# First mixer of a two-layer block: scans in a fixed tensor-engine order of fourteen steps, convolution evictions recorded ahead of the step

## The chip, the cores and the metric

The kernel runs on one NeuronCore of a Trainium2 chip. The metric is the device time of one execution in microseconds (us). The profile names the engines PE (TensorE, matmuls), PEld (its weight loads), DVE (VectorE), ACT (ScalarE), POOL (GpSimd) and SP (SyncE, here only a queue that issues DMAs).

## What is computed

The reference is a block of two layers: a state-space mixer, then an attention mixer, each followed by a mixture of experts. The change lies in the state-space mixer alone, which works on 512 latent tokens and 256 context tokens (T = 768, six chunks of 128; chunks 0 to 3 are latent, 4 and 5 context):

```
z, xbc, dtr = split(u @ in_w)                    # input projection
xbc = silu(conv5(xbc));  xs, Bm, Cm = split(xbc) # centred convolution of 5 taps
dt  = softplus(dtr + dt_bias);  acum = cumsum(dt * A)       # per chunk and direction
y_diag = ((Cm Bm^T) * exp(acum_l - acum_s) * tri) @ (dt * xs)
states = Bm^T @ (exp(acum_end - acum) * dt * xs)
h      = exp(acum_end) * h + states               # from chunk to chunk
y      = y_diag + (Cm * exp(acum)) @ h_prev       # forward and backward, summed
out    = rmsnorm((y + D * xs) * silu(z)) @ out_w
```

There are 8 groups of 4 heads, of 64 values each, and a forward and a backward scan in every group.

## The kernel before

`ssd` runs eight groups. For each, `ssd_in` projects six column tiles of 128 (B, C, x0, x1, z0, z1). A tile's fp32 weights come by DMA (SP), are split into a high part (`split`, L445, ACT) and a low part (L446, POOL), and `mm3` (L475 to L477) issues three matmuls for each of 8 slices of the input: 24 matmuls of 256 columns for the context half (PSUM tile `pin`), then 24 of 512 for the latent half. `pin` takes three PSUM banks in turn, so the first half of a tile can only start when the half tile three places earlier has been evicted. The eviction of B, C, x0 and x1 is the convolution: one ACT activation (L808) and four dependent DVE operations (L813) per half, then a tanh (L814) and a product (L816). z0 and z1 need one tanh and one DVE operation per half.

While group g+1 is projected, the scan of group g advances. `ssd_group` is a Python generator; `between`, called twice a tile, lets it run to its next `yield` and in every second call also runs one step of a filler (L544: eight matmuls for the modulation vectors, in groups 0 to 3 until they are used up). The generator's parts are `transposed(c)` (rows of x and B of a chunk by PE transposes, copied by ACT into `rowx`), `state(i)` (PE matmul into `st`, new state `hst` by DVE), `prepare(c)` (decay matrices: DMA `ab`, POOL L865, DVE L867, ACT exp L868 give `m`; `ce` is the decayed C; the PE product `cb` is masked into `cbm` by DVE L877 and L878, weighted by ACT L882 and DVE L883 and multiplied by `m` in L884, giving `w`), `product(c)` (24 or 16 small matmuls into the PSUM tile `y`, L902) and `ssd_out` (L945 and L946 on DVE, then a DMA).

The order of instructions on each engine is made by the framework's scheduler from the order of recording and its own estimates; the kernel fixes the order on PE only in other stages. After the eighth group the scan of the last group runs beside the context part of the output projection `ssd_proj`.

Of the kernel before, what the change touches and what calls it, by code (L numbers as in the profile page):

```python
# [22 lines left out]
P = 128  # L23
D = 1024
KT = 8
S = 512
# [353 lines left out]
class Kern:  # L380
# [225 lines left out]
    def ssd(self, e0, esc, rest):  # L606
# [7 lines left out]
        with ExitStack() as so:  # L614
# [13 lines left out]
            k = {nm: kp.tile([P, 6, 64], F32, name=nm) for nm in ("dt", "dtd", "acum", "dec")}  # L628
# [17 lines left out]
            inner = iter(())  # L646

            def between(i):
                next(inner, None)
                if i % 2:  # L650
                    next(filler, None)

            for g in range(8):
                cz = self.ssd_in(g, wp, gp, pp, (hhi, hlo), k, between)
                if g == 0:
                    self.ssd_dt(gp, wp, pp, (hhi, hlo), k, aS)
                for _ in inner:
                    pass
                inner = self.ssd_group(g, gp, pp, k, *cz)
# [9 lines left out]
            for n, _ in enumerate(inner):  # L669
                if n:  # L670
                    next(proj)
# [26 lines left out]
    def ssd_dt(self, tp, wp, pp, h, K, aS):  # L698
# [3 lines left out]
        dt, dtd, acum, dec, tle, tge = (K[n] for n in ("dt", "dtd", "acum", "dec", "tle", "tge"))  # L702
# [37 lines left out]
        nc.scalar.copy(acum, pa)  # L740
        pt = pp.tile([P, 6, 64], F32, name="ptot", tag="y")
# [19 lines left out]
    def ssd_in(self, g, wp, gp, pp, h, K, between):  # L761
# [20 lines left out]
        for i, nm in enumerate(names):  # L782
            if i in early:
                between(False)
                between(True)
# [3 lines left out]
            for a, b in ((S, T), (0, S)) if i not in early else ():  # L789
# [5 lines left out]
                between(a == 0)  # L795
            th = gp.tile([P, T], F32, name="th", tag="th", bufs=1)
            if nm[0] == "z":
                z = gp.tile([P, T], F32, name="zs", tag="zs", bufs=4)
                for p_, a, b, n in seg:
                    nc.scalar.activation(th[:, a:b], p_, AF.Tanh, scale=0.5)  # L800
                    nc.vector.scalar_tensor_tensor(z[:, a:b], th[:, a:b], 1.0, p_, op0=ALU.add, op1=ALU.mult)
                zs[nm] = z
                continue
            ct = ctile[nm]
            tap = lambda j: cwh[:, j * 32 + ct:j * 32 + ct + 1]
            acc = gp.tile([P, T], F32, name="acc", tag="acc", bufs=2)
            for p_, a, b, n in seg:
                nc.scalar.activation(acc[:, a:b], p_, AF.Identity, scale=tap(2), bias=cwh[:, 160 + ct:161 + ct])  # L808
                for j in (0, 1, 3, 4):
                    s = j - 2  # L810
# [9 lines left out]
    def ssd_group(self, g, gp, pp, K, conv, zs):  # L820
# [84 lines left out]
        for c in (4, 5, 0):  # L905
            transposed(c)
# [1555 lines left out]
```

## Time and profile before

| | |
|---|---|
| runs | 3304.07, 3310.75, 3310.1 us; median 3310.1 us |
| profiled execution | 3311.26 us, of which the span of the core is 3309.5 us |
| groups 0 to 7 of the mixer, from the first input matmul | 36.1 to 679.9 us of the span |
| tail of the mixer, last scan beside the context projection | 679.9 to about 773 us |

In the rows below a "form" is the shape of an instruction, `x` a count; "busy" is the union of the intervals, "mean ns" the length of one instruction, and "idle before" the time its engine waited and for whom. Matmul lengths overlap; the distance between two starts is what one costs.

### The profile page before, as it was taken

Reading aid. Unit: us, or ns where it says so; the run is one execution under the profiler, and the core shown is the slowest. Engines: PE = TensorE matmul, PEld = TensorE weight load, DVE = VectorE, ACT = ScalarE, POOL = GpSimd, SP = SyncE. Lnnn points to the kernel's source line nnn. Section 1 sums busy time; section 2 is a strip of 40 time slices with the busy share of each in tenths; the row PEclk is TensorE's granted clock in tenths of the full one; section 3 lists DMA queues with packets and bytes.
Section 4 is the critical chain, followed back from the end, with each engine's and each line's share of the span. In section 5 each row is a group of like instructions: output and inputs, shape, how many; then the busy total and the mean of one; then the engine's idle time right before and its main releaser. Section 6 shows DMA issues by size and latency. Waiting matters only on the chain.

```text
span 3309.5 us, 47859 instructions
## 1 busy us (share of the span) xinstructions
PE 3129.0 (95%) x18944; PEld 2070.5 (63%) x18944; DVE 1638.5 (50%) x3014; ACT 1165.6 (35%) x2063; POOL 965.6 (29%) x694
## 2 busy tenths in 40 slices
PE   7999998889999999999999899999999999999998
PEld 4677777777754343434757644434467778988886
DVE  5588888887522121114466410004379864763312
ACT  4344444455511111114567410001154354662222
POOL 1344545554210000002601200000154443145543
PEclk9999999989999999999999999999999999999999
DMA  7355433355488989894252589999832224443332
GB/s 253 125 165 163 143 89 92 101 163 163 127 304 329 358 323 369 318 367 148 83 185 67 219 326 409 409 400 398 324 118 80 80 65 150 134 158 100 96 92 86
DMA packets 234416, 668.60 MB, mean 202 GB/s; under 512 B 19344, under 2 KB 73488, under 8 KB 229840
## 3 DMA queue, kind: packets, MB, share of 16 engines
q1 hardware_dynamic: 224240, 645.43, 54.2%
q10 hardware_dynamic: 9952, 20.12, 1.9%
q8 instruction: 149, 2.44, 0.3%
q14 instruction: 75, 0.61, 0.1%
HBM read 651.65 MB, written 13.83 MB: 201 GB/s over the span
## 4 chain that ended last, share of the span: by engine, by line
PE 60%; DVE 8%; DMA 5%; ACT 2%; issue 2%; POOL 1%; SPq 0%; DVEq 0%; ACTq 0%; POOLq 0%
PE mm L475 7%; PE mm L476 7%; PE mm L477 7%; PE py L1102 3%; PE pg L1102 3%; PE pa L1102 3%; PE pa L1313 3%; PE py L1266 3%; PE pg L1313 2%; DMA wm<-in_moe_w_dram 2%; PE gth L343 2%; PE cy L1104 2%; PE cg L1104 2%; PE ca L1104 2%; DMA raw<-in_moe_w_dram 1%
## 5 line engine op out<-in xcount | busy, mean ns | idle before, releaser
L446 POOL TENSOR_TENSOR wlo<-raw,whi 128x1024 fp32r<-128x1024 f32 (+3 forms) x207 | 461.2, 2230 | 634.3 <-ACT whi L445 600.9
L445 ACT CAST whi<-raw 128x1024 fp32r<-128x1024 f32 (+2 forms) x291 | 285.7, 984 | 477.7 <-PE mm L476 200.8
L475 PE MATMUL mm<-stk,whi 128*128 128x512 f32 (+2 forms) x944 | 342.6, 363 | 0.0
L477 PE MATMUL mm<-stk,wlo 128*128 128x512 f32 (+2 forms) x944 | 335.9, 356 | 0.0
L476 PE MATMUL mm<-stk,whi 128*128 128x512 f32 (+2 forms) x944 | 335.1, 355 | 0.0
L475 PE MATMUL pin<-hhi,whi 128*128 128x256 f32 (+1 forms) x768 | 271.2, 354 | 4.0 <-DVE acc L813 3.8
L477 PE MATMUL pin<-hhi,wlo 128*128 128x256 f32 (+1 forms) x768 | 265.2, 345 | 0.0
L476 PE MATMUL pin<-hlo,whi 128*128 128x256 f32 (+1 forms) x768 | 263.3, 343 | 0.0
L58 POOL TENSOR_TENSOR sqa<-sqa,sq 128x256 f32<-128x256 f32 (+1 forms) x56 | 64.7, 1155 | 467.6 <-PE py L1266 408.5
L475 PEld LDWEIGHTS mm<-stk,whi 128*128 128x128 f32 (+1 forms) x944 | 179.7, 190 | 33.1 <-issue 7.9
L1166 POOL TENSOR_TENSOR cT<-cT,scc 128x256 f32<-128x256 f32 x56 | 39.6, 738 | 544.5 <-ACT scc L1165 543.7
L476 PEld LDWEIGHTS mm<-stk,whi 128*128 128x128 f32 (+1 forms) x944 | 179.6, 190 | 29.9 <-issue 6.2
L477 PEld LDWEIGHTS mm<-stk,wlo 128*128 128x128 f32 (+1 forms) x944 | 179.3, 190 | 26.1 <-issue 1.1
L475 PEld LDWEIGHTS pin<-hhi,whi 128*128 128x128 f32 x768 | 146.4, 191 | 45.9 <-issue 19.6
L1188 DVE TENSOR_TENSOR ac<-ac,pg 128x512 f32<-128x512 f32 x16 | 11.0, 687 | 300.4 <-PE pg L1102 300.4
L476 PEld LDWEIGHTS pin<-hlo,whi 128*128 128x128 f32 x768 | 146.5, 191 | 18.7 <-issue 1.7
L477 PEld LDWEIGHTS pin<-hhi,wlo 128*128 128x128 f32 x768 | 146.3, 190 | 18.3 <-issue 1.7
L813 DVE SCALAR_TENSOR_TENSOR acc<-pin,cwh,acc 128x511 f32<-128x511 f32 (+3 forms) x256 | 148.5, 608 | 14.3 <-ACT acc L808 12.6
L1345 DVE TENSOR_TENSOR ac<-ac,pg 128x512 f32<-128x512 f32 x16 | 11.0, 687 | 248.1 <-PE pg L1313 248.1
L867 DVE SCALAR_TENSOR_TENSOR m<-ab,acum,m 128x128 f32<-128x128 f32 x192 | 115.3, 643 | 25.3 <-POOL m L865 25.3
L446 DVE TENSOR_TENSOR wlo<-raw,whi 128x1024 fp32r<-128x1024 f32 (+1 forms) x84 | 105.0, 1254 | 40.7 <-ACT whi L445 40.0
L872 POOL TENSOR_TENSOR ce<-ce,xc 128x1024 f32<-128x1024 f32 (+1 forms) x48 | 103.4, 2154 | 39.8 <-ACT ce L871 36.0
(716 smaller groups left out, 7184.7 us busy)
## 6 DMA issues: line engine op xcount, KB each, us to landing
wm<-in_moe_w_dram SPq DMA_DIRECT2D x227, 1024.0 KB, 9.5
raw<-in_moe_w_dram SPq DMA_DIRECT2D x186, 512.0 KB, 8.9
raw<-in_ada_w_dram SPq DMA_DIRECT2D x96, 512.0 KB, 4.8
raw<-in_moe_w2h_dram SPq DMA_DIRECT2D x76, 512.0 KB, 8.9
raw<-in_w_f_dram SPq DMA_DIRECT2D x68, 512.0 KB, 3.6
wm<-in_moe_w2h_dram SPq DMA_DIRECT2D x26, 1024.0 KB, 8.3
raw<-in_w_ssd_in_dram SPq DMA_DIRECT2D x48, 512.0 KB, 4.6
ab<-aS SPq DMA_DIRECT2D x96, 256.0 KB, 4.7
```

The costliest lines, as they stand in the source:

```text
L445: nc.scalar.copy(hi[:, 0:n], raw[:, 0:n])
L446: (eng or self.lo).tensor_tensor(lo[:, 0:n], raw[:, 0:n], hi[:, 0:n].bitcast(F32), op=ALU.subtract)
L475: nc.tensor.matmul(ps, wh, ah, start=start, stop=False)
L476: nc.tensor.matmul(ps, wh, al, start=False, stop=False)
L477: nc.tensor.matmul(ps, wl, ah, start=False, stop=stop)
L813: nc.vector.scalar_tensor_tensor(o, p_[:, lo + s:hi + s], tap(j), o, op0=ALU.mult, op1=ALU.add)
L867: nc.vector.scalar_tensor_tensor(m[:, r, :], ab[:, r, :], acum[:, c, 4 * g + r:4 * g + r + 1], m[:, r, :], op0=ALU.subtract, op1=ALU.min)
L872: nc.gpsimd.tensor_tensor(ce[:, j0:j1, :], ce[:, j0:j1, :], conv["C"][:, o:o + P].unsqueeze(1).to_broadcast([P, j1 - j0, P]), op=ALU.mult)
L1102: nc.tensor.matmul(pb[z][o:o + 32, :], lb(k, e)[:, 32 * h:32 * h + 32], w[e][k % 2][:, z * 512:(z + 1) * 512], tile_position=(0, o), **f)
L1104: nc.tensor.matmul(pc[o:o + 32, :], ls(k, e), w[e][k % 2][:, h * 512:(h + 1) * 512], tile_position=(0, o), **f)
L1266: nc.tensor.matmul(py[64 * e:64 * e + 64, :], aT[:, k, 64 * e:64 * e + 64], w[e][a], start=(k == 0), stop=(k == KT - 1), tile_position=(0, ...
L1313: nc.tensor.matmul(pb[hf][64 * e:64 * e + 64, :], lb(k, e), w[e][a][:, hf * 512:(hf + 1) * 512], tile_position=(0, 64 * e), **f)
```

## The change

- The scan has fourteen steps. The first twelve run beside the next group's six tiles, the last two beside the first tile of the group after that, so `inner` is a list of generators. In groups 1 to 7 PE's order is that of recording (`manual_schedule`). Fillers stand at steps 1, 3, 5, 7, 9 and 11.
- A tile's eviction is recorded ahead of the step behind its latent half; before, both steps of a tile were recorded ahead of it.
- `prepare` becomes `begin` for two chunks together: (4, 5), (1, 2), (0, 3). Their products stand three or four steps later.
- Work moves from DVE to ACT: of the four L867 per chunk the subtraction becomes four ACT activations with a pointer bias, in place in `ab`, and one `tensor_tensor` of 512 columns takes the minimum. The state's eight products per step become eight ACT copies of 64 columns with a pointer scale (`hsc`), and both directions are added in one DVE operation of 512 columns. `cbm` is masked for two chunks at once.
- `nacum` (the negated `acum`) is computed once. The scaled rows `xdd` are made one step ahead of their state.

```diff
+            def scans():
+                for z in list(inner):
+                    if next(z, inner) is inner:
+                        inner.remove(z)
+
+            def between():
+                nonlocal step
+                scans()
+                if step in FILL:
                     next(filler, None)
+                step += 1
...
+                with tc.manual_schedule(engines={mybir.EngineType.PE}) if g else ExitStack():
+                    cz = self.ssd_in(g, wp, gp, pp, (hhi, hlo), k, between)
...
-                inner = self.ssd_group(g, gp, pp, k, *cz)
+                inner.append(self.ssd_group(g, gp, pp, k, *cz))
...
+            scans()
+            while inner:
+                scans()
+                next(proj)
...
-                between(a == 0)
...
+                if a:
+                    between()
+            self.ssd_evict(nm, seg, ctile.get(nm), gp, cwh, conv, zs)
+            between()
...
+            hn = gp.tile([P, 512], F32, name="hst", tag="hst", bufs=5)
...
+                nc.vector.tensor_tensor(hn, hsc[0], ps, op=ALU.add)
...
+                    nc.scalar.activation(hsc[0][:, o:o + 64], hn[:, o:o + 64], AF.Copy, scale=dec[:, c, col:col + 1])
...
             for r in range(4):
-                nc.vector.scalar_tensor_tensor(m[:, r, :], ab[:, r, :], acum[:, c, 4 * g + r:4 * g + r + 1], m[:, r, :], op0=ALU.subtract, op1=ALU.min)
+                nc.scalar.activation(ab[:, r, :], ab[:, r, :], AF.Identity, bias=nacum[:, c, 4 * g + r:4 * g + r + 1])
+            nc.vector.tensor_tensor(m, ab[:, 0:4, :], m, op=ALU.min)
...
+            for z, t in enumerate((tle, tge)):
+                nc.vector.tensor_tensor(cb[:, z], p2, t.unsqueeze(1).to_broadcast([P, 2, P]), op=ALU.mult)
...
+        transposed(4)
+        transposed(5)
         yield
+        transposed(0)
+        transposed(3)
+        scaled(0)
+        yield
         state(0)
+        begin(4, 5)
+        scaled(1)
         yield
         state(1)
+        scaled(2)
+        transposed(1)
         yield
+        transposed(2)
+        yield
+        product(4)
+        product(5)
         state(2)
+        begin(1, 2)
+        yield
+        self.ssd_out(g, gp, yctx, S, C, conv, zs)
+        scaled(3)
         yield
         state(3)
+        scaled(4)
         yield
         state(4)
         yield
+        product(1)
+        product(2)
+        begin(0, 3)
         yield
+        yield
+        yield
         yield
         product(0)
         product(3)
         self.ssd_out(g, gp, ylat, 0, S, conv, zs)
```

PE in group 1, where the step sizes have just been computed (`ptot` ends that computation, `st` is the first state of the first scan). Before:

```order
L738 MATMUL pa<-dt_la,tle 128x6x32
L739 MATMUL pa<-dt_la,tge 128x6x32
L742 MATMUL ptot<-dt_la,ones 128x384
L477 MATMUL pin<-hhi,wlo 128x256
L475 MATMUL pin<-hhi,whi 128x256
```

After:

```order
L746 MATMUL pa<-dt_la,tle 128x6x32
L747 MATMUL pa<-dt_la,tge 128x6x32
L751 MATMUL ptot<-dt_la,ones 128x384
L865 MATMUL st<-xdd,rowx 128x256 x2
L902 MATMUL cb<-xc 128x128 x2
L475 MATMUL pin<-hhi,whi 128x512
```

Before, the rest of a context half and most of a latent half stood between `ptot` and the first `st`; now `st` follows at once.

DVE in a later group, around `begin(1, 2)`; the L828 rows of 254 and 255 columns are the convolution of x1's context half, those of 510 and 511 of its latent half. Before (L867 is the decay of one chunk, L813 the convolution):

```order
L813 SCALAR_TENSOR_TENSOR acc<-pin,cwh,acc 128x254
L813 SCALAR_TENSOR_TENSOR acc<-pin,cwh,acc 128x510
L867 SCALAR_TENSOR_TENSOR m<-ab,acum,m 128x128 x4
L816 SCALAR_TENSOR_TENSOR xc<-th,acc 128x768
L877 TENSOR_TENSOR cbm<-cb,tle 128x128
L878 TENSOR_TENSOR cbm<-cb,tge 128x128
```

After:

```order
L831 SCALAR_TENSOR_TENSOR xc<-th,acc 128x768
L893 TENSOR_TENSOR m<-ab,m 128x512 x2
L912 SCALAR_TENSOR_TENSOR w<-cbm,dt,w 128x128 x2
L990 SCALAR_TENSOR_TENSOR yo<-yo,zs 128x256
L912 SCALAR_TENSOR_TENSOR w<-cbm,dt,w 128x128 x3
L913 TENSOR_TENSOR w<-w,m 128x512
L912 SCALAR_TENSOR_TENSOR w<-cbm,dt,w 128x128 x3
L828 SCALAR_TENSOR_TENSOR acc<-pin,cwh,acc 128x254
L913 TENSOR_TENSOR w<-w,m 128x512
L828 SCALAR_TENSOR_TENSOR acc<-pin,cwh,acc 128x255
```

Before, the work on one chunk stood behind a finished eviction; now x1's convolution stands behind the weights of two chunks.

## Rows read from the trace of the kernel before

**Rows 1.** The page, part 1: busy time and share of the span.

```profile
PE 3129.0 (95%) x18944; PEld 2070.5 (63%) x18944; DVE 1638.5 (50%) x3014; ACT 1165.6 (35%) x2063; POOL 965.6 (29%) x694
```

**Rows 2.** Busy time by stretch: groups 1, 2, 3, 4 to 7, and the tail.

```profile
core 0: us, PE busy (x) PEld busy (x) DVE busy (x) ACT busy (x) POOL busy (x), PEclk, DMA share, GB/s
113.20:208.20 95.00, 86.83 (x557) 63.62 (x555) 75.28 (x164) 41.81 (x77) 41.59 (x31) 0.96 0.47 150
208.20:289.60 81.40, 76.64 (x519) 60.60 (x517) 67.54 (x156) 34.80 (x65) 40.83 (x29) 0.98 0.50 156
289.60:373.30 83.70, 78.52 (x519) 60.49 (x515) 67.69 (x152) 34.83 (x66) 39.48 (x28) 0.96 0.51 163
373.30:679.90 306.60, 279.20 (x1850) 238.59 (x1848) 263.05 (x597) 135.79 (x256) 156.93 (x111) 0.96 0.32 95
679.90:773.20 93.30, 76.53 (x614) 69.45 (x615) 78.55 (x153) 50.06 (x99) 43.39 (x44) 0.93 0.61 198
```

**Rows 3.** The same stretch of groups 4 to 7, instructions on `pin` alone.

```profile
373.30:679.90 306.60, 223.12 (x1152) 180.92 (x1152) 82.58 (x144) 29.17 (x48) 0.96 0.32 95
```

**Rows 4.** Timeline of PE: a 512-column half behind a wait, and one without.

```profile
350.03 0.76 PE L475 MATMUL pin<-hhi,whi 128*128 128x512 f32 x1 [3.79 <-DVE acc L813]
...
357.97 0.44 PE L902 MATMUL y<-w,rowx 128*64 128x128 f32 x4
...
365.13 0.50 PE L475 MATMUL pin<-hhi,whi 128*128 128x512 f32 x1
...
370.83 0.44 PE L902 MATMUL y<-w,rowx 128*64 128x128 f32 x4
...
372.29 0.64 PE L544 MATMUL ada<-raw,sc 128*32 128x512 f32 x4
```

**Rows 5.** Timeline of PE: a filler, a 256-column half, a product.

```profile
256.72 1.06 PE L544 MATMUL ada<-raw,sc 128*32 128x512 f32 x8
257.71 0.38 PE L475 MATMUL pin<-hhi,whi 128*128 128x256 f32 x1
...
260.74 0.44 PE L902 MATMUL y<-w,rowx 128*64 128x128 f32 x4
```

**Rows 6.** Waits between engines, groups 4 to 7: total us, times, longest.

```profile
PE y L902 <- DVE w L884: 20.5, 4, 6.3
```

**Rows 7.** Instruction groups by form, groups 4 to 7.

```profile
L867 DVE SCALAR_TENSOR_TENSOR m<-ab,acum,m 128x128 f32<-128x128 f32 x96 | 50.1, 567 | 11.4 <-POOL m L865 11.4
L883 DVE SCALAR_TENSOR_TENSOR w<-cbm,dt,w 128x128 f32<-128x128 f32 x96 | 39.5, 467 | 0.1
L882 ACT ACTIVATE w<-cbm,dt 128x128 f32<-128x128 f32 x96 | 30.5, 388 | 12.3 <-DVE cbm L877 12.3
L852 DVE SCALAR_TENSOR_TENSOR hst<-hst,dec,st 128x64 f32<-128x64 f32 x128 | 28.3, 275 | 5.8 <-PE st L845 5.3
L884 DVE TENSOR_TENSOR w<-w,m 128x512 f32<-128x512 f32 x24 | 16.3, 681 | 0.0
L877 DVE TENSOR_TENSOR cbm<-cb,tle 128x128 f32<-128x128 f32 x24 | 6.7, 281 | 0.0
L848 DVE COPY hst<-st 128x256 f32<-128x256 f32 x8 | 3.4, 425 | 15.4 <-PE st L845 15.4
```

**Rows 8.** Timeline of DVE: the same operation beside POOL's work and alone.

```profile
412.53 3.29 DVE L867 SCALAR_TENSOR_TENSOR m<-ab,acum,m 128x128 f32<-128x128 f32 x4
...
420.44 0.87 DVE L867 SCALAR_TENSOR_TENSOR m<-ab,acum,m 128x128 f32<-128x128 f32 x3
```

**Rows 9.** Instruction groups by form, whole run: the nearest ACT form of 64 columns.

```profile
L294 ACT ACTIVATE af<-af 128x64 f32<-128x64 f32 x2 | 0.5, 257 | 0.4 <-DVE af L293 0.4
```

**Rows 10.** Timeline of PE, group 1: from the sums of the step sizes to the first states.

```profile
131.89 0.81 PE L742 MATMUL ptot<-dt_la,ones 128*128 128x384 f32 x2
...
138.46 0.70 PE L845 MATMUL st<-xdd,rowx 128*128 128x256 f32 x2 [0.38 <-POOL xdd L844]
```

**Rows 11.** Instruction groups by form on DVE, tail (679.9 to 773.2 us).

```profile
L867 DVE SCALAR_TENSOR_TENSOR m<-ab,acum,m 128x128 f32<-128x128 f32 x16 | 11.4, 764 | 0.0
```

More of the change, by code (lines that the diff above doesn't have):

```diff
@@ L627, in ssd @@
             nc.vector.tensor_scalar(cwh, self.v("cw", 0, 192), 0.5, None, op0=ALU.mult)
-            k = {nm: kp.tile([P, 6, 64], F32, name=nm) for nm in ("dt", "dtd", "acum", "dec")}
+            k = {nm: kp.tile([P, 6, 64], F32, name=nm) for nm in ("dt", "dtd", "acum", "nacum", "dec")}
             k.update(tle=tle, tge=tge, cwh=cwh, aV=aS.rearrange("(d g r) c l -> g c d r l", d=2, g=8))
@@ L877, in prepare @@
-            nc.vector.tensor_tensor(cb[:, 0, :], pb[:, 0:P], tle, op=ALU.mult)
-            nc.vector.tensor_tensor(cb[:, 1, :], pb[:, 0:P], tge, op=ALU.mult)
-            w = gp.tile([P, 4, P], F32, name="w", tag="w", bufs=2)
-            for r in range(4):
-                f, b = [dt[:, c, d * 32 + 4 * g + r:d * 32 + 4 * g + r + 1] for d in range(2)]
-                nc.scalar.activation(w[:, r, :], cb[:, 0, :], AF.Copy, scale=f)
-                nc.vector.scalar_tensor_tensor(w[:, r, :], cb[:, 1, :], b, w[:, r, :], op0=ALU.mult, op1=ALU.add)
@@ L884, in prepare, with weights @@
-            nc.vector.tensor_tensor(w, w, m, op=ALU.mult)
-            prep[c] = (w, ce)
+            half[c] = m, ce, j0, j1
+        def weights(cs):
+            pb = pp.tile([P, 512], F32, name="cb", tag="aux")
+            cb = gp.tile([P, 2, 2, P], F32, name="cbm", tag="cbm", bufs=1)
+            for i, c in enumerate(cs):
+                o = off(c)
+                nc.tensor.matmul(pb[:, i * P:(i + 1) * P], conv["B"][:, o:o + P], conv["C"][:, o:o + P], start=True, stop=True)
+            p2 = pb[:, 0:256].rearrange("p (i l) -> p i l", i=2)
+            for z, t in enumerate((tle, tge)):
+                nc.vector.tensor_tensor(cb[:, z], p2, t.unsqueeze(1).to_broadcast([P, 2, P]), op=ALU.mult)
+            for i, c in enumerate(cs):
+                m, ce, _, _ = half.pop(c)
+                w = gp.tile([P, 4, P], F32, name="w", tag="w", bufs=2)
+                for r in range(4):
+                    f, b = [dt[:, c, d * 32 + 4 * g + r:d * 32 + 4 * g + r + 1] for d in range(2)]
+                    nc.scalar.activation(w[:, r, :], cb[:, 0, i, :], AF.Copy, scale=f)
+                    nc.vector.scalar_tensor_tensor(w[:, r, :], cb[:, 1, i, :], b, w[:, r, :], op0=ALU.mult, op1=ALU.add)
+                nc.vector.tensor_tensor(w, w, m, op=ALU.mult)
+                prep[c] = (w, ce)
```

140 lines of the change are left out of this document (61 added, 79 removed).

## The prediction

> **What bounds the kernel now.** Over the whole span PE is busy 95% and no other engine over 50% [rows 1]; so I first asked for the busy time by stretch, the stretches being the groups of the first mixer. There the picture differs: in groups 4 to 7 a group takes 306.60 / 4 = 76.65 us, PE is busy 69.8 of them, DVE 65.8 and ACT 33.9, and the granted clock is 0.96 [rows 2]. Two engines are nearly full, one of them in order behind the other. Then I asked what PE does with its time. Matmuls on `pin` are 223.12 / 4 = 55.8 us of a group [rows 3], so the small matmuls are 14.0. Without a wait a 512-column half takes 5.70 us from its first start to the next instruction [rows 4] and a 256-column half 3.03 [rows 5]: a tile is 8.73, six are 52.4. The floor of a group is therefore 52.4 + 14.0 = 66.4 us, and 10.25 us of the 76.65 are waits and what follows them. The waits are PE's on DVE: the product waits for the weights `w` [rows 6], or a half tile for the eviction that frees its bank. What follows one: the half behind the wait of 3.79 us took 7.94 us in place of 5.70 [rows 4], its matmuls starting at the lower of the two clock levels. So in these groups the end is set by DVE's order of work and by the clock lost behind it. A microsecond saved here should reach the end: the stages behind begin when the mixer has ended.
>
> **DVE's work.** Removed from a group, out of the four groups' busy time [rows 7]: L867 50.1 / 4 = 12.5, L852 28.3 / 4 = 7.1, L848 0.85, and two masks (L877 and its like at L878) 13.4 / 4 = 3.35; together 23.8. Added: six minima of 512 columns, not in the trace. The nearest form is L884, an SBUF-only operation of 512 columns: 0.68 each, 4.1 in all. One state copy and four additions of 512 columns, 0.68 by the same row: 3.4. Six masks of 256 columns, nearest L848 of 256: 0.425 each, 2.55. Sum 10.05. DVE goes from 65.8 to 52.05 a group. The upper bound of a minimum comes from L867 itself: four took 3.29 beside POOL's work, three 0.87 alone [rows 8], so 2.1 more for the four columns' worth, and a minimum may cost 2.8. I take 0.68, because it is one instruction with one start in place of four.
>
> **ACT's work.** 24 activations of 128 columns with a pointer operand: L882 is that form, 30.5 / 96 = 0.32 each [rows 7], 7.6. 32 copies of 64 columns: between 0.257 [rows 9] and L882's 0.388; I take 0.26, the shorter tile's, 8.3. ACT goes from 33.9 to 49.8, still under the floor of 66.4, so it adds nothing by its sum, only through order. L882's 388 ns for 128 columns shows how little the columns matter. The Trainium skill ("ScalarE: Activation LUTs", section "What ACT_TABLE_LOAD costs") gives an activation with a pointer operand 280 ns + 0.833 ns a column, which is 387 ns at 128, and the trace agrees; by it a 64-column copy would be 333 ns and ACT would stand at 52.2 us. That speaks against moving work in such small pieces, but leaves ACT below PE.
>
> **The order on PE.** The small matmuls stay, as do the fillers, POOL's operations and the loads (`ab` four quarters as before, now for two chunks together; SP issues them between weight loads, and `ab` comes free only after the minimum). These cost nothing while PE has tiles in front of it; the cover is the three or four half tiles between a `begin` and its products. What changes is where PE can wait, since matmuls now stand in a fixed line. Take the stretch from the end of B's latent half to the start of z0's latent half. PE's work in it: two latent products at 1.46 (370.83 to 372.29 [rows 4]) 2.9, two context products 2.0, three tiles 26.2, z0's context half 3.0, three quarters of the other small matmuls (14.0 - 4 x 1.46 - 2.0 = 6.2) 4.7; 38.8. z0's latent half needs the bank of x1's context half, whose convolution now stands behind the weights of chunks 1 and 2 on DVE. DVE must do by then all its 52.05 but the weights of chunks 0 and 3 (2 x (4 x 0.41 + 0.68 + 0.68) + 0.85 = 6.9), one state (0.7) and about a fifth of its 20.6 on `pin` (4.1): 40.35. It also waits for POOL, 11.4 / 4 = 2.85 a group at L867 [rows 7]. 43.2 against 38.8: PE waits 4.4 us at this half, and I charge 2.0 for the clock behind it (2.24 behind the row's 3.79). The rest of the group, some 28 us on PE, holds little more than 12 on DVE, so no second wait.
>
> **The sum.**
> - Groups 4 to 7: 66.4 + 4.4 + 2.0 = 72.8 against 76.65, 4 x 3.85 = 15.4 us gained.
> - Groups 2 and 3 hold six fillers of 0.99 [rows 5], 5.9; four stand in the crowded stretch and cover 4.0 of the 4.4. 66.4 + 5.9 + 1.0 (what is left, and some clock) = 73.3, against 81.4 and 83.7: 8.1 + 10.4 = 18.5.
> - Group 1: 66.4 + 5.9 + 3.3 for the sums of step sizes, less 2.9 (two products go to the next group) = 72.7. Now `st` stands directly behind `ptot`; the last of its inputs let it start at 138.46, 5.8 us after `ptot` ended [rows 10], and nothing is between. I charge 5.7 + 2.2 clock, and 2.8 for a second wait at the first weights (0 to 8). 83.4 against 95.0: 11.6.
> - Tail: DVE is busy 78.55 of 93.3 [rows 2]. It loses L867's 11.4 [rows 11], 6.9 and 3.3 for masks and copies of states at the groups' prices and 0.9 more, and gains 10.05: 12.4 less. I take 8, since the projection's own row loads and two products of group 6 stay in it.
> - Group 0 and `nacum` (one DVE operation): nothing.
>
> Together 53.5. From the profiled execution's 3311.3 us (the median of the runs is 3310.1, 1.2 lower) that makes **3258 us**. Its ends: no wait at all leaves 4 x 10.25 + 9.1 + 11.4 + 22.3 + 12.4 = 96, 3215 us; the other end is given by the next case.
>
> **Rival 1, faster but less: DVE waits out POOL.** L867 took 0.82 a piece beside POOL and 0.29 alone [rows 8]. If every minimum pays the 2.1 us in full, three in the crowded stretch add 6.3 to the wait there: 25 us in groups 4 to 7 and 12 in 2 and 3, so 3295 us. For it: L867's mean of 567 [rows 7] shows that it paid about half of that on average. Against: one long operation meets POOL once, not four times. The Trainium skill ("SBUF — State Buffer", section "Who interferes with whom") says that a DVE instruction with two SBUF inputs contends with a GpSimd one that reads SBUF; by that the minimum would be caught and the state's addition, one input of which is in PSUM, would not. The trace agrees for L867, and has no row of the minimum.
>
> **Rival 2: the waits move and stay as long.** The product no longer waits, but z0's half waits 8 us and the clock takes 2.2: 10.25 again, in every group; only the tail's gain or less is left, 3303 to 3311 us. For it: both evictions and weights are still in one DVE line. Against: 13.7 us less work in that line.
>
> **Rival 3, slower: the fixed line is too short for the chain.** From `begin(1, 2)` to its products PE has two tiles, 17.5 us, and some states. The chain behind it goes from ACT (bias, 8 x 0.32) to DVE (minima) to ACT (exp, weights) to DVE, 11 us by itself. If the two queues also serve evictions and states in turn between its links (x0's and x1's, 5 us each on DVE, the context output and a state 6), it is 28: PE waits 10.5 at the product, then 4.4 at z0's half, with the clock twice 2.2: 19.3 over the floor, 85.7 a group. That is 36 us more in groups 4 to 7, 10 in 2 and 3, nothing gained in 1, 8 gained in the tail: 3349 us. It decides where the waits of a group pass 10.25. For it: ACT and DVE would both be about 50 of 66 us full. Against: PE's work in the line is longer than either's sum. That the change does not do what it says I rule out: the order shows the fixed line and the operations moved.
>
> **How the numbers follow.** About 0.2%, 6.6 us, is what a measurement of this kernel can tell from no change. The forecast has 0.53, its best end (under 3225) 0.10, rival 1 0.19, rival 2 0.08, rival 3 0.10. Rival 2 counts as the same; faster is 0.82, slower 0.10. The range of 8 in 10 runs from 3222 to 3303: it holds the forecast's case and rival 1, and leaves out the best end's lower part, most of rival 2 and rival 3.
>
> **What would show it.** Groups 4 to 7 near 73 us a group with DVE near 52 and ACT near 50; PE's longest waits at `pin` for DVE's convolution, once a group, and in group 1 a wait of 5 to 6 us at `st`. L893 near 0.68 (over 1.4 means rival 1). Wrong would be: PE's largest wait at a product for DVE's `w`, twice as long as now; or groups shorter but the tail or the stage behind longer by the same amount.

## The result and the profile after

The change makes the kernel faster, by less than half of the forecast: 3288.4 us (median of 4 runs, 3283.7 to 3291.3) against 3310.4 beside it (4 runs, 3304.1 to 3311.7), a ratio of 0.9928, 95% interval [0.9913, 0.9942]; 22 us gained where 53 were forecast. The profiled execution took 3291.3 us, its span is 3289.5 against 3309.5.

| us | before | after | gained | forecast |
|---|---|---|---|---|
| group 0 | 77.1 | 78.7 | -1.6 | 0 |
| group 1 | 95.1 | 84.7 | 10.4 | 11.6 |
| groups 2 and 3 | 165.0 | 147.2 | 17.8 | 18.5 |
| groups 4 to 7 | 306.6 | 296.0 | 10.6 | 15.4 |
| end of `pin` to end of the latent projection | 217.7 | 227.4 | **-9.7** | **8** |
| from there to the end of the span | 2411.9 | 2420.2 | -8.3 | 0 |

(The rest, 0.8 us, is an earlier start of group 0.) The same stretches as in [rows 2], now of the changed kernel; the columns are those of its first line:

```profile
core 0: us, PE busy (x) PEld busy (x) DVE busy (x) ACT busy (x) POOL busy (x), PEclk, DMA share, GB/s
114.00:198.70 84.70, 76.02 (x508) 60.19 (x506) 68.25 (x106) 55.94 (x134) 40.80 (x29) 0.98 0.47 145
198.70:272.50 73.80, 73.29 (x522) 59.02 (x518) 59.98 (x105) 49.28 (x123) 41.82 (x29) 1.00 0.61 188
272.50:345.90 73.40, 72.89 (x518) 58.64 (x514) 56.70 (x95) 48.46 (x120) 41.02 (x28) 1.00 0.56 180
345.90:641.90 296.00, 274.23 (x1874) 237.81 (x1871) 227.60 (x384) 193.25 (x480) 163.02 (x112) 0.97 0.34 100
641.90:735.20 93.30, 74.84 (x582) 69.01 (x580) 66.23 (x99) 60.92 (x146) 40.74 (x45) 0.84 0.56 184
```

In groups 4 to 7 DVE is busy 56.9 us a group (65.8 before) and ACT 48.3 (33.9 before). Groups 2 and 3 run at a clock of 1.00, and PE waits 1.0 us in them in all. In the first 93.3 us behind `pin` DVE is busy 12.3 us less, as forecast, yet less is done at their end: ACT is busy 10.9 more, and the granted clock fell from 0.93 to 0.84.

PE's waits in groups 4 to 7 (us in total, times, longest):

```profile
PE rp L850 <- DVE hst L870: 12.0, 4, 3.8
PE pin L475 <- DVE acc L828: 8.1, 4, 2.1
```

The wait for `w` of [rows 6] is gone. The wait at `pin` is the one I forecast, once a group, but 2 us long; a second, at the transposes of chunk 2 (`rp`), I had not seen. In PE's timeline it comes first:

```profile
447.48 0.90 PE L850 MATMUL rp<-ident,xc 128*128 128x128 f32 x3 [3.76 <-DVE hst L870]
448.04 0.78 PE L475 MATMUL pin<-hhi,whi 128*128 128x512 f32 x1
448.61 0.63 PE L476 MATMUL pin<-hlo,whi 128*128 128x512 f32 x1
...
455.96 0.40 PE L477 MATMUL pin<-hhi,wlo 128*128 128x512 f32 x1
456.29 0.44 PE L931 MATMUL y<-w,rowx 128*64 128x128 f32 x4
```

The half tile behind it takes 448.04 to 456.29, 8.25 us, where one without a wait takes 5.70 [rows 4]: 2.55 us of clock. A matmul of 512 columns takes 0.63 us at its start and 0.40 at its end; the granted clock is 0.50 from 448.04 to 453.3 and 1.00 behind that. Behind a wait of 2.06 us at z0's latent half (399.99) the clock did not fall. Why `rp` waits, DVE's timeline shows:

```profile
441.14 0.69 DVE L913 TENSOR_TENSOR w<-w,m 128x512 f32<-128x512 f32 x1
...
443.99 2.18 DVE L913 TENSOR_TENSOR w<-w,m 128x512 f32<-128x512 f32 x1
446.10 0.74 DVE L828 SCALAR_TENSOR_TENSOR acc<-pin,cwh,acc 128x511 f32<-128x511 f32 x1
446.76 0.67 DVE L870 TENSOR_TENSOR hst<-hsc,st 128x512 f32<-128x512 f32 x1
```

`rp` takes the bank of the second state, which the addition at L870 frees; it stands in DVE's line behind the weights of chunks 4 and 5 and a convolution. Of the two products with `m` in front of it (L913) the second took 2.18 us in place of 0.69, beside this split of weights on POOL:

```profile
443.13 2.50 POOL L446 TENSOR_TENSOR wlo<-raw,whi 128x1024 fp32r<-128x1024 f32 x1
```

So some 1.5 of the 3.76 us of this wait come from that one slow operation (an estimate from the two lengths); it is as slow in groups 6 and 7.

The operations of groups 4 to 7 (busy us, mean ns of one), beside [rows 7] and [rows 9]:

```profile
L912 DVE SCALAR_TENSOR_TENSOR w<-cbm,dt,w 128x128 f32<-128x128 f32 x96 | 41.8, 484 | 1.5 <-ACT w L911 0.9
L878 ACT ACTIVATE hsc<-hst,dec 128x64 f32<-128x64 f32 x128 | 33.0, 335 | 31.0 <-DVE hst L870 26.9 <-DVE hst L868 4.1
L892 ACT ACTIVATE ab<-ab,nacum 128x128 f32<-128x128 f32 x96 | 30.6, 392 | 0.1
L893 DVE TENSOR_TENSOR m<-ab,m 128x512 f32<-128x512 f32 x24 | 24.3, 1024 | 1.4 <-POOL m L890 1.4
L913 DVE TENSOR_TENSOR w<-w,m 128x512 f32<-128x512 f32 x23 | 23.6, 1025 | 0.2
L870 DVE TENSOR_TENSOR hst<-hsc,st 128x512 f32<-128x512 f32 x16 | 10.8, 678 | 0.9 <-ACT hsc L878 0.9
```

And PE's waits from the end of `pin` to the end of the context's projection:

```profile
PE y L931 <- DVE w L913: 15.4, 3, 6.1
```

### The profile page after: what moved, and what is told of

It reads as the page before. It is cut to its first block, busy times and chain, and to the rows that moved or that the text cites. A ratio compares the mean times of both kernels' runs of the same rounds, so it can differ in the third digit from the quotient of the medians.

```text
span 3289.5 us, 47744 instructions
## 1 busy us (share of the span) xinstructions
PE 3119.5 (95%) x18944; PEld 2071.9 (63%) x18944; DVE 1571.1 (48%) x2591; ACT 1280.7 (39%) x2511; POOL 971.2 (30%) x694
## 4 chain that ended last, share of the span: by engine, by line
PE 59%; DVE 9%; DMA 5%; ACT 2%; issue 2%; POOL 1%; SPq 0%; ACTq 0%; DVEq 0%; POOLq 0%
PE mm L475 6%; PE mm L476 6%; PE mm L477 6%; PE py L1146 3%; PE pg L1146 3%; PE pa L1146 3%; PE py L1310 3%; DMA wm<-in_moe_w_dram 3%; PE pa L1357 2%; PE pg L1357 2%; PE cy L1148 2%; PE cg L1148 2%; PE gth L343 2%; PE ca L1148 2%; DMA raw<-in_moe_w_dram 1%
## 5 line engine op out<-in xcount | busy, mean ns | idle before, releaser
L475 PEld LDWEIGHTS mm<-stk,whi 128*128 128x128 f32 (+1 forms) x944 | 180.7, 191 | 33.5 <-issue 8.2
L828 DVE SCALAR_TENSOR_TENSOR acc<-pin,cwh,acc 128x254 f32<-128x254 f32 (+3 forms) x256 | 151.1, 611 | 64.6 <-ACT acc L823 62.0
L1357 PE MATMUL pa<-wm,xxg 128*64 128x512 f32 x416 | 108.7, 597 | 1.9 <-DMA wm<-in_moe_w_dram 1.9
L1357 PE MATMUL pg<-wm,xxg 128*64 128x512 f32 x368 | 103.6, 596 | 4.0 <-DMA wm<-in_moe_w_dram 4.0
```

Of the source, the lines that this page charges most:

```text
L475: nc.tensor.matmul(ps, wh, ah, start=start, stop=False)
L828: nc.vector.scalar_tensor_tensor(o, p_[:, lo + s:hi + s], tap(j), o, op0=ALU.mult, op1=ALU.add)
L1357: nc.tensor.matmul(pb[hf][64 * e:64 * e + 64, :], lb(k, e), w[e][a][:, hf * 512:(hf + 1) * 512], tile_position=(0, 64 * e), **f)
```

## The experiments

All times beside runs of the kernel before on the same chip; "tail" is from the end of `pin` to the end of the latent projection, in the profiled execution.

| run | us, median | ratio to before, 95% interval | end of `pin` | tail |
|---|---|---|---|---|
| changed kernel | 3288.4 | 0.9928 [0.9913, 0.9942] | 641.9 | 227.4 |
| e8 the same again | 3286.5 | 0.9931 [0.9919, 0.9944] | 643.6 | 227.4 |
| e4 operations alone | 3296.3 | 0.9964 [0.9952, 0.9976] | 653.5 | 228.2 |
| e3 eviction behind | 3285.7 | 0.9933 [0.9921, 0.9945] | 643.7 | 226.9 |
| e7 no fixed order | 3280.9 | 0.9912 [0.9899, 0.9926] | 640.4 | 228.0 |
| e2 `rp` later | 3289.9 | 0.9942 [0.993, 0.9954] | 644.5 | 227.9 |
| e5 and evicted by halves | 3285.8 | 0.9933 [0.992, 0.9945] | 641.1 | 229.7 |
| e9 and begin(1, 2) later | 3279.1 | 0.9905 [0.9891, 0.9918] | 629.8 | 231.4 |
| e1 last group by single chunks | 3288.3 | 0.994 [0.9928, 0.9953] | 641.1 | 226.8 |
| e6 last scan earlier | 3290.3 | 0.9944 [0.9931, 0.9958] | 650.5 | 222.7 |
| e10 projection ahead | 3285.6 | 0.9923 [0.991, 0.9937] | 642.4 | 228.0 |
| e13 DVE's line | 3285.4 | 0.9932 [0.9917, 0.9947] | 640.2 | 226.0 |
| e14 and ACT's line | 3287.2 | 0.9938 [0.9925, 0.9951] | 645.1 | 227.8 |
| e15 last group's operations old | 3273.9 | 0.9895 [0.988, 0.991] | 644.5 | 221.6 |
| e16 only its decays old | 3289.4 | 0.9945 [0.9932, 0.9957] | 644.9 | 226.2 |
| e18 only its states old | 3277.0 | 0.9901 [0.9884, 0.9918] | 640.0 | 216.6 |
| e11 e9 and e10 | 3273.9 | 0.989 [0.9876, 0.9903] | 628.2 | 230.7 |
| e12 e11, no fixed order | 3269.9 | 0.988 [0.9867, 0.9894] | 628.9 | 229.5 |
| e17 e9, no fixed order, last group old | 3265.9 | 0.9873 [0.986, 0.9887] | 624.7 | 223.5 |

### What of the change carries the groups

**e4, the operations alone**, in the old twelve steps:

```diff
-                with tc.manual_schedule(engines={mybir.EngineType.PE}) if g else ExitStack():
+                with ExitStack():
...
+            between()
             self.ssd_evict(nm, seg, ctile.get(nm), gp, cwh, conv, zs)
-            between()
...
+            scaled(1)
+            state(1)
+            begin(4)
+            yield
...
+            state(3)
+            begin(5)
+            yield
```

> The operations of the change alone (bias on ACT and one minimum, states of both directions in one, copies of scaled states on ACT, masks as in the change but for one chunk at a time) in the order of the kernel before: twelve steps, one chunk at a time, evictions behind the step, no fixed order on PE. Theory O (what DVE is rid of carries the gain, as my forecast's sum by DVE says): groups 4 to 7 take 72 to 75 us in place of 76.65, and the tail is 8 us shorter: 3270 to 3290. Rival P (the order carries it; DVE's lighter line only waits more for ACT, whose line is now in the chain of every chunk): groups 4 to 7 at 76 us or more, 3300 or more.

Neither alone. Groups 4 to 7 took 294.1 us, as short as in the changed kernel (Theory O holds there), but groups 1 to 3 took 92.0, 77.0 and 77.1 against 84.7, 73.8 and 73.4, and no gain came in the tail. In groups 5 to 7 PE still waits for `w`, 3.2 us a group:

```profile
PE y L934 <- DVE w L916: 9.6, 3, 3.9
PE rp L852 <- ACT rowx L854: 3.9, 3, 1.3
```

More than half of e4's gain in groups 4 to 7 is group 7 alone (69.1 us, its wait for `w` 1.8 us; 75.1 in the changed kernel). Groups 4 to 6 took 75.0 each, against 76.8 before and 73.6 in the changed kernel. So the operations give the larger part of groups 4 to 7, and the order adds 14 us in groups 1 to 3.

**e3, the evictions behind the step:**

```diff
-            self.ssd_evict(nm, seg, ctile.get(nm), gp, cwh, conv, zs)
             between()
+            self.ssd_evict(nm, seg, ctile.get(nm), gp, cwh, conv, zs)
```

> The changed kernel with the evictions behind the step again, as before, all else as changed. Theory E (where the eviction stands sets PE's waits for banks, since DVE and ACT work in order): the convolutions stand behind weights and states, the waits at `pin` for DVE's convolution grow from 2.0 us a group to 5 or more with the clock behind them, and groups 4 to 7 take 77 to 80 us in place of 74.0: the time rises by 15 to 30 us, to 3303 to 3318. Rival F (the fixed order of PE carries the change, the place of the eviction does not): groups 4 to 7 within 1.5 us of 74.0, the time within 5 us of 3288.

Rival F in its numbers; its reason, the fixed order, is taken up by e7. The wait at `rp` fell to 1.9 and that at `pin` rose to 3.6 us: the sum of both is the same, 5.6 against 5.8, and so are the groups (298.7 against 296.0 in all four).

**e7, without the fixed order** (the first line of e4's diff alone):

> The changed kernel without the fixed order of PE in groups 1 to 7: the scheduler places the small matmuls among those of `pin`. Theory X (the fixed line is what takes the wait for `w` away and what brings the waits at the bank of `rp`): the 3.8 us at `rp` are gone, and waits for `w` at `y` of 3 us or more are back in groups 4 to 7, which stay within 2 us of 74.0 each; the time 3284 to 3292. Rival Y (the steps and the eviction make the order by themselves, the fixed line adds nothing): the order of waits is the same and the time within 2 us of the changed kernel's. If the fixed line itself is worth much, groups 1 to 3 lose 3 us or more each and the time is over 3294.

Rival Y in the order of the waits: 3.5 us at `rp` and 1.5 at `pin`, none for `w`; groups 4 to 7 took 294.1, groups 1 to 3 233.1 (231.9 with the fixed line). Its time of 3280.9 us was 5.6 below that of the changed kernel on the same chip (e8), which neither theory had; the intervals of the two ratios overlap. The fixed line is not what takes the wait for `w` away; with the eviction's place ruled out by e3, the fourteen steps are left (no run drops both at once).

### The wait in groups 4 to 7

**e2, the transposes of chunk 2 one step later:**

```diff
-        transposed(2)
         yield
+        transposed(2)
         product(4)
```

> The changed kernel with one line moved: the transposes of chunk 2 (`rp`) stand one step later, ahead of the products of chunks 4 and 5, so that their bank, which the addition of the second state (L870) frees, is asked for a half tile later. Theory R (this wait of 3.8 us, and the 2.6 us that the half tile behind it takes longer, is a wait for a bank and nothing else): groups 5 to 7 take 68 to 70 us in place of 74.6 to 75.1, and the time falls by 12 to 18 us, to 3270 to 3276. Rival D (my forecast's sum: DVE is full from the context output to x1's convolution, so that PE's next wait, at z0's latent half, grows by what is saved here, from 2.0 to 6 to 8 us): groups 5 to 7 within 1.5 us of where they were, the time within 4 us of 3288.

Half of each. The wait at `rp` is gone with its clock (Theory R), and z0's latent half now waits for what it hid (Rival D); the groups' times lie between the two:

```profile
PE pin L475 <- DVE acc L828: 14.1, 3, 4.7
```

That is the 4.4 us of the forecast, at the place it named, and groups 5 to 7 took 72.2, 71.9 and 73.5 (forecast 72.8). The gain there went again in groups 2 and 4, which now wait at the same half (4.1 and 3.7 us).

**e5, each half tile evicted as soon as it is done** (on e2):

```diff
-                seg.append((ps, a, b, b - a))
+                self.ssd_evict(nm, [(ps, a, b, b - a)], ctile.get(nm), gp, cwh, conv, zs)
                 if a:
                     between()
-            self.ssd_evict(nm, seg, ctile.get(nm), gp, cwh, conv, zs)
+            if seg:
+                self.ssd_evict(nm, seg, ctile.get(nm), gp, cwh, conv, zs)
...
```

> The kernel with the later transposes of chunk 2, in which groups 5 to 7 took 72 us and PE waited once a group, 4.7 us at z0's latent half for DVE's convolution of x1's context half; here each half tile is evicted as soon as its matmuls have ended, not both halves behind the latent one, so that this convolution is in DVE's line some 6 us earlier. Theory L (the bank is held by the place of the convolution in the line): the wait of 4.7 us is gone or under 1 us and groups 5 to 7 take 67 to 69 us, the mixer's `pin` ends 10 to 18 us earlier than at 644.5. Rival M (DVE's sum in the stretch sets it: the convolution is ready earlier but the line behind it is late, and PE waits as long for a product or the next bank): groups 5 to 7 within 1.5 us of 72.

This tells nothing between the two: in DVE's timeline the convolution stood at the same place behind the weights as in e2, since what is written earlier need not be ordered earlier there. The wait stayed at 4.6.

**e9, begin(1, 2) one step later** (on e5):

```diff
-        begin(1, 2)
         yield
         self.ssd_out(g, gp, yctx, S, C, conv, zs)
         scaled(3)
+        begin(1, 2)
         yield
```

> The kernel with evictions by halves and the later transposes of chunk 2, in which DVE's order was still the same and PE waited 4.6 us at z0's latent half; here the weights of chunks 1 and 2 are begun one step later, so that x1's context convolution stands ahead of all their products with `dt` on DVE (the order shows it, at last), with 16 us of PE's work still between them and their products. Theory K (place in the line: the convolution waits behind 5 us of weights): the wait at z0's latent half falls under 1 us and groups 5 to 7 take 68 to 70 us in place of 72.8 to 74.0. Rival M (DVE is full there, whatever stands first): the wait moves to `y` of chunks 1 and 2 for `w`, 3 to 6 us, and groups 5 to 7 stay within 1.5 us of 73.

Half of each. The wait at z0's half fell to 0.9 us or none, `pin` ended 11.3 us earlier than in e5, but most of that in groups 1 to 4; in groups 5 to 7 (72.3, 71.8, 71.9) waits of 2.4 us at the next `pin` for z1's eviction and of 1.5 at `y` came up. The place in DVE's line decides where PE waits; DVE is busy 63.1 of 72 us a group there (189.4 in groups 5 to 7), more than the 56.9 of the changed kernel, though its operations are the same: the one at L912 took 652 ns on average in place of 484.

### The tail

**e1, the last group in the old twelve steps, one chunk at a time:**

```diff
+        if g == 7:
+            for c in (4, 5, 0):
+                transposed(c)
+            yield
...
+            state(1)
+            begin(4)
+            yield
```

> The changed kernel, but the scan of the last group, which runs beside the projection's steps behind the end of `pin`, takes the old twelve steps and begins one chunk at a time. Theory T (the new order of steps is too short there: a projection step holds only 3.1 us of matmuls, so the weights of two chunks are begun two or three such steps ahead of their products and PE waits 3.6, 5.7 and 6.1 us at `y` and runs its next 70 to 100 matmuls on a lower clock): the last `y` comes about 69 us after the end of `pin` as in the kernel before, in place of 82.6, and the time falls by 10 to 14 us, to 3275 to 3279. Rival S (the sum of ACT's and DVE's work in the tail, 67 and 74 us of 105, sets it in any order): the waits move to other places, the last `y` stays within 3 us of 82.6, the time within 4 us of 3288.

Theory T to the last `y` (69.6 us after `pin`), Rival S in the time: the context's projection ended 3.5 us earlier, the latent one 0.6. **e6, the last scan three steps earlier**, beside its own z tiles:

```diff
+            if g == 7 and nm == "z0":
+                start(conv, zs)
             between()
```

> The changed kernel, but the last group's scan starts beside its own z0 and z1 tiles, three steps earlier, one chunk at a time, so that only nine of its steps are left for the tail (the group before it runs its last products two steps earlier to free the buffers). Theory T (the tail is a chain of latencies, begin to product and state to state, and no engine's sum): the last `y` comes 55 to 60 us after the end of `pin` in place of 82.6, the projection of the context ends some 10 us earlier, and the time is 3275 to 3281. Rival S (what is left in the tail by work, ACT's 67 and PE's 87 us of 105, sets the end of the context's projection): the last `y` comes earlier, but the projection ends within 4 us of where it did, or group 7 grows by as much, and the time stays at 3284 to 3290.

Rival S: the last `y` came after 55.2 us, group 7 took 84.8 in place of 75.1, with a wait of 4.3 at `st` for POOL.

**e10, two more projection steps ahead of the routing, e13 and e14, DVE's and then also ACT's line written down** (all on e1; the diff is that of e13, e14 names ACT beside DVE, e10 only lets the loop run fourteen times):

```diff
-            while inner:
+            for _ in range(12):
                 scans()
                 next(proj)
-            st.close()
-            xT, R = rest(cT)
+            with tc.manual_schedule(engines={mybir.EngineType.DVE}):
+                for _ in range(3):
+                    i0 = next(proj)
+                st.close()
+                xT, R = rest(cT)
```

> The kernel whose last group begins one chunk at a time, with all fourteen plain steps of the context's projection ahead of the routing's first operations, two more than there were. In that kernel the 13 us won at the last `y` shrank to 4 at the end of the context's projection: ACT's line stood 9.4 us at the routing's first copy, which takes memory that the last store of `yo` had to leave, with the casts of the next weights behind it, PE waited 4.2 us for them and went on at a clock of 0.85. Theory U (it is this line): no wait over 2 us at `po` after the last `y`, and the projection ends 25 to 28 us after the last `y` in place of 32; the time 4 to 7 us less than 3288. Rival V (the projection's own rows and casts are late at that place anyway): 30 us or more, the time within 3 us.

> The kernel whose last group begins one chunk at a time, and DVE's line of the last projection steps written down: the rows and weight splits of the context's projection, up to its first finished output, stand ahead of the routing's first operations, which wait for the memory that the last store of `yo` leaves. Theory W (DVE's line behind that store keeps the projection late): after the last `y` the wait of 3.6 to 4.2 us at `po` is gone, the next 96 matmuls take 13 to 15 us in place of 20, and the projection ends 25 to 28 us after the last `y`, 94 to 97 us after `pin`; the time 3278 to 3283. Rival V (the rows and weights themselves arrive late there): 30 us or more after the last `y`, a wait of 3 us or more at `po` for another operand, the time within 3 us of 3287.

> The same with ACT's line written down as well, so that its casts and rows stand ahead of the routing's first copy too. Theory W: as with DVE's line alone or 1 to 3 us better, 92 to 96 us from the end of `pin` to the end of the context's projection, and no wait over 1.5 us at `po`. Rival V: within 2 us of the run with DVE's line alone, with the wait at `po` for a load or its split.

e10 came out as Rival V in its numbers: the projection ended 33.5 us after the last `y`. DVE, not ACT, held PE: its first routing operation waited 4.5 us for the memory of the last store of `yo`, PE waited 3.6, and the first 96 projection matmuls behind the last `y` took 20.0 us with that wait. e13 removed exactly that (no wait, 13.7 us, the context's projection ended 94.7 us after `pin`; Theory W), but the time of 3285.4 is Rival V's, since the latent projection still ended after 226.0: from the context's end to its own it took 131.3 us (122.2 before), with waits inside it for the routing that was put back. So neither the steps nor these lines alone set the tail. e14 was no better (98.5 us to the context's end).

**e15, e16, e18: the last group's operations.** On e1, its decays, its states, or both as they were:

```diff
+                if g < 7:
                     nc.scalar.activation(ab[:, r, :], ab[:, r, :], AF.Identity, ...
+                else:
+                    nc.vector.scalar_tensor_tensor(m[:, r, :], ab[:, r, :], acum[...], m[:, r, :], op0=ALU.subtract, op1=ALU.min)
...
+            if g == 7:
+                        nc.vector.scalar_tensor_tensor(hn[:, o:o + 64], hsc[0][:, o:o + 64], dec[...], ps[:, o:o + 64], op0=ALU.mult, op1=ALU.add)
```

> The changed kernel, but the last group has the old steps and the old operations (four subtract-and-minimum on DVE, states with their decay on DVE), so that the tail is the old one but for two products of the group before. Theory Q (the work moved to ACT makes the tail longer, since ACT has the projection's casts and rows there as well): from the end of `pin` to the end of the latent projection 217 to 221 us, and the time 3277 to 3282. Rival Z (what ends before the tail decides, such as the carried product or the clock at its start): 225 to 229 us as in all kernels with the new operations, and the time 3284 to 3290.

> As that, but only the decays of the last group are the old ones (7.6 us of ACT's work goes back to DVE), the states stay new (8.3 us of copies stay on ACT, in the chain from state to state). Theory Q with the decays at fault: 218 to 222 us, as with both. Theory Q with the states at fault (eight copies stand between one state and the next): 224 to 228 us. If both share it: 221 to 225. Rival Z: 225 to 229, as with both.

> The last group with the old steps and the old states (decay and addition in one operation on DVE, no copies on ACT), its decays new (bias on ACT, one minimum on DVE). If the states' copies on ACT lengthen the tail: 220 to 223 us from the end of `pin` to the end of the latent projection, as with both old, and the time 3274 to 3282. If the two only act together: 225 to 228 us, and 3284 to 3290.

The tail in one row each (columns as above): before, e1, e16, e15, e18.

```profile
679.90:897.60 217.70, 198.15 (x1182) 160.67 (x1183) 159.00 (x272) 118.53 (x210) 86.76 (x80) 0.96 0.52 164
```

```profile
641.10:867.90 226.80, 206.12 (x1208) 164.95 (x1207) 154.14 (x236) 133.74 (x265) 90.67 (x82) 0.95 0.50 160
```

```profile
644.90:871.10 226.20, 199.43 (x1206) 161.17 (x1205) 159.37 (x255) 127.66 (x244) 89.71 (x82) 0.96 0.51 160
```

```profile
644.50:866.10 221.60, 204.13 (x1208) 164.49 (x1207) 164.79 (x283) 120.06 (x212) 91.70 (x82) 0.96 0.50 164
```

```profile
640.00:856.60 216.60, 200.50 (x1209) 160.79 (x1208) 156.87 (x266) 126.34 (x233) 89.41 (x82) 0.98 0.52 168
```

With the states' decay back on DVE the tail is 216.6 (shorter than expected), with both old 221.6; with the states new it is 226.2 and 226.8, whatever the decays. The medians part the same way: 3277.0 and 3273.9 against 3289.4 and 3288.3. So the loss goes with the states. How they cause it is not shown. In e1's timeline of ACT the eight copies stand between one state's addition and the next, among the projection's rows and casts:

```profile
652.95 1.03 ACT L445 CAST whi<-raw 128x1024 fp32r<-128x1024 f32 x1
654.06 0.59 ACT L878 ACTIVATE hsc<-hst,dec 128x64 f32<-128x64 f32 x2
...
654.56 1.53 ACT L878 ACTIVATE hsc<-hst,dec 128x64 f32<-128x64 f32 x6
655.99 1.27 ACT L912 ACTIVATE w<-cbm,dt 128x128 f32<-128x128 f32 x4
657.16 2.01 ACT L878 ACTIVATE hsc<-hst,dec 128x64 f32<-128x64 f32 x8
659.08 0.49 ACT L1071 ACTIVATE yh<-yt,vecs 128x256 fp32r<-128x256 f32 x1
```

But PE waited only 0.6 us for a state in e1, and the last `y` came 69.6 us after `pin`, as before (69.1). The loss comes behind it, where no state is left: to the context's end 32.0 us in e1 and 36.1 in e16, against 26.5 before, 27.3 in e15 and 29.0 in e18. From the last `y` to the context's end, before and in e1:

```profile
748.90:775.40 26.50, 23.56 (x187) 22.15 (x186) 19.14 (x34) 13.47 (x24) 7.68 (x15) 1.00 0.76 242
```

```profile
710.70:742.70 32.00, 27.63 (x187) 25.81 (x188) 20.74 (x37) 14.45 (x26) 10.32 (x17) 0.84 0.66 223
```

There ACT's first copy of the routing waited in e1 for the landing of the last store of `yo`:

```profile
ACT xrb L238 <- DMA yS<-yo: 9.4, 1, 9.4
```

This wait was 10.0 us in e16, 0.2 in e15, and is absent before and in e18. In e1 and e16 that copy stands two casts of the projection's weights earlier in ACT's line than in the other three. So a rival to the copies' place between the states is left: that the new operations only led the scheduler to start the routing too early. Against it, e13 and e14, which have no such wait on ACT or DVE, kept a tail of 226.0 and 227.8. No run fixed this order with the new and the old states.

### The stages behind, and the repairs together

**e8, the changed kernel again:**

> The changed kernel once more, to see how much of the 8 us that the stages behind the mixer took longer (2420.2 us from the end of the latent projection to the end of the span, against 2411.9 in the kernel before; 2409.9 to 2416.5 in the four experiments so far, all with the same program there) belongs to the change. Theory N (nothing: short drops of the granted clock come at other places in each execution): 2410 to 2417 us here. Rival C (an earlier end of the mixer makes them longer): 2418 us or more again. The mixer should repeat within 1 us: `pin` ends at 641 to 643, the last `y` at 724 to 726.

2416.5 us, at the upper end of Theory N's range; `pin` ended at 643.6, 1.7 us later than in the first profile. Over the eighteen experiments this stretch, with the same work in all, took 2409.9 to 2420.4 (mean 2414.5), with no trend by when the mixer ended (2415.9 in the earliest, e17). Of the 8.3 us that the changed kernel's profile lost there, 2.6 separate the one profile of the kernel before from that mean and may belong to the change; the rest lies within the scatter. The drops of the granted clock come at other places: in the 20 us that begin 300 us behind DVE's last write to `cT` it was 0.91 in the changed kernel and 1.00 in e1 and e3.

**e11, e12, e17** (e9 with e10; also without the fixed order; e9 without it, with e15's last group):

> Evictions by halves, later transposes of chunk 2, weights of chunks 1 and 2 one step later, and the last group one chunk at a time with the projection's steps ahead of the routing: both repairs in one kernel. They touch different stretches, so I expect their sum: `pin` ends as in the kernel with the groups' repair alone (630 to 636 if it works, 641 if not), the context's projection ends 95 to 98 us later (105.1 in the changed kernel), and the time is 3268 to 3278. If the stages behind give it back, as the 4 us of the last group's repair were given back, 3282 or more.

> The same as the kernel with both repairs, without the fixed order of PE in groups 1 to 7. The changed kernel without it took 3280.9 us against 3286.5 on the same chip, its mixer 1 to 3 us less. Theory Y (the steps make the order, the fixed line is worth nothing or costs 1 to 3 us): the groups within 1 us each of those with the fixed line, the time 0 to 5 us less. Rival X (the fixed line now carries something): the groups longer by 2 us or more each, the time 8 us or more above.

> The kernel with evictions by halves, later transposes, later begin and no fixed order, its last group with old steps and old operations. Theory Q: its groups stay as they were (`pin` ends at 629), the latent projection ends 217 to 222 us later, at 846 to 851, and the time is 3258 to 3265. Rival Z: 226 to 230 us, 3267 to 3272.

The times of e11 and e12 came as expected (groups alike, 73.1 and 72.7 for 2 and 3 in both), but in e11 the context's projection ended 105.2 us after `pin`, not 95 to 98: all of its gain is the groups'. e17 is the fastest, 43 us less than before and some 20 less than the changed kernel; its tail of 223.5 and its time lie between Theory Q and Rival Z. The same with only the states old was not tried.

## Why the prediction was partly wrong

- **The sign and the range held, the size did not**: the forecast's sum is 53.5, the two profiles differ by 20.0. Of the 33.5 missing, the groups are 7.5 (38.0 at the end of `pin` for 45.5), the tail 17.7, the stages behind 8.3.
- **The step that failed is the tail's term**: "Tail: DVE is busy 78.55 of 93.3 ... 12.4 less. I take 8". DVE did lose 12.3 us there, but a stretch in which an engine is 84% busy need not be set by its sum. I priced ACT's added work by the floor of a group ("adds nothing by its sum, only through order") and used that in a stretch with another floor: in the tail ACT also makes the projection's rows and casts, and each state now passes through it. It measured -9.7 us, where 8 were to be gained. Giving the last group its old states back brings the tail from 226.8 to 216.6, and from 226.2 to 221.6 where its decays are old too: the states carry half of the loss or all of it; by which way stays open. The prediction had named such an end as a sign of being wrong, groups shorter but the tail longer; the tail lost a quarter of what the groups had gained.
- **Groups 1 to 3**: right (28.2 gained of 30.1). In group 1 the wait at `st` was 3.0 us in place of 5.7, for POOL's `xdd`; others at the sums of step sizes (2.6 and 1.8) made up for it.
- **Groups 4 to 7**: the mechanism right, the size short: 74.0 in place of 72.8, 4.8 us in all. The forecast had one wait, 4.4 us at z0's latent half and 2.0 of clock. In groups 5 to 7 of the changed kernel `rp` waits 3.76 and costs 2.55 of clock, and 2.0 are left at z0. e2 moved the one line, and the forecast's wait and group length came out. What I missed is that the steps put every bank's next user at a place of its own, with the fixed line or without it (e7 waits 3.5 us at `rp` too), and that each has to be followed, not only `pin`'s.
- **DVE 52.05 forecast, 56.9 measured**: the minimum 1.02 for 0.68, L913 1.02 for 0.68 and L912 41.8 us busy for 39.5 are 2.1, 2.1 and 0.6 us a group, nearly the whole difference. That is Rival 1's mechanism at a sixth of its price for a minimum (0.34 in place of 2.1), and not at the minimum alone. The forecast's 0.68 held for the 13 of 24 minima that met no work of POOL (0.68 to 0.69); the 11 that met some took 1.10 to 2.18. By the Trainium skill ("SBUF — State Buffer", section "Who interferes with whom") the operations with two SBUF inputs are caught and the state's addition with one input in PSUM is not; the trace agrees: 1.02 against 0.678, and the addition took 0.67 to 0.69 with POOL's work beside it or without. Meeting POOL is not enough, though: six of the 24 operations L884 before ran beside it and took 0.68 all the same; what decides is open.
- **ACT 49.8 forecast, 48.3 measured**: right. The 128 copies of 64 columns kept ACT busy for 33.0 us, 0.26 each, as I had taken by the nearest row. One of them lasts 335 ns, and it overlaps the next; the estimate by the Trainium skill ("ScalarE: Activation LUTs", section "What ACT_TABLE_LOAD costs") was 333, and the trace agrees. Summed over a row of copies that overlap (52.2 us for ACT), it was too high.
- **Rival 2** (the waits move) is right in kind where my "no second wait" failed: the changed kernel waits at two places, 5.8 us a group, and in e9 at others again; its size, 10.25 in every group, did not come. Rival 3 did not come: no product waits in groups 4 to 7.
- **"The stages behind begin when the mixer has ended"**: they do; up to 2.6 of the 8.3 us may be the change's, and the rest lies within the scatter of single executions.

## What to carry to other kernels

An engine's sum is a bound only for the stretch in which it was counted: where work moves to another engine, count that engine anew in every stretch the moved work reaches, the last one above all, where the next stage's work has begun. Here the states, moved to ACT, made the last stretch 4.6 to 10.2 us longer, though ACT was busy only 59% of it; try such a move stretch by stretch. And where work changes its step, follow each buffer's next user to the place where it now stands, and look there for operations that another engine's work makes slow.

## What the hardware showed that was not expected

- Behind a wait of 3.76 us a half tile took 8.25 us, behind one of 2.06 us 5.68 (399.99 to the next instruction at 405.67, in the changed kernel): the shorter wait cost its own length, the longer one two thirds more. These are two places; no run varied the length of a wait alone.
- An operation of DVE with two SBUF inputs (L913) took from 0.68 to 2.80 us for the same 512 columns in groups 4 to 7: 0.68 to 0.69 where POOL did nothing, 1.20 to 2.80 beside its work.
- The same program behind the mixer took 2409.9 to 2420.4 us in eighteen profiles, more than the difference that some of the experiments were to show.
